# Weight-part buffers 64 bytes longer, and half the software DMA scratch, in a two-layer hybrid trunk

## The chip, the core and the metric

The kernel runs on one core of a Trainium2 chip. Its time is the device time of one launch in microseconds, the median of three runs: 2938.9 us (2937.18 to 2940.47). On the core, TensorE (PE) multiplies matrices, VectorE (DVE) and ScalarE (ACT) work element by element, GpSimd (POOL) and SyncE (SP) here issue transfers. SBUF is the working memory of 128 partitions, and an address below is a byte offset within a partition. PSUM is the memory that TensorE writes.

## The reference

Each of two layers takes x of 256 tokens by 2048 features, all in float32, and computes

```
h  = rms_norm(x);  [c_q | c_kv,k_pe | u | gates] = h @ W_in
a  = latent attention(c_q, c_kv, k_pe), 16 heads, block-causal, then @ w_o
s  = GLU(gelu(diagonal state-space scan of u))         # S5, 64 groups x 64 states
m  = sigmoid(g_a) * a + sigmoid(g_b) * s
x  = x + rms_norm(m @ W_out)
x  = x + rms_norm((silu(h2 @ W_gate) * (h2 @ W_up)) @ W_down),  h2 = rms_norm(x)
```

The hidden width of the last line is 5632. All weights of a layer are read once.

## The kernel before, in words

All products with weights keep the activations stationary (128 features by 128 tokens are loaded into the array as `lhsT`) and stream the weights (`rhs`, 128 rows by 512 columns). float32 accuracy is had from three products of a type called float32r: each operand is split into a high and a low part, and the result is high·high + high·low + low·high. `gemm` (from line 413 of the kernel before) issues these three for every 128 features and each of the two blocks of 128 tokens; lines 444, 445 and 446 are the three matmuls, with the moving operands `hi`, `lo`, `hi`. Before each matmul stands its weight load (row PEld in the trace).

The weights come through class `Weights`. A tile is 128 partitions by 1024 float32 (two slices of 512 columns): SP fetches it into `raw` (4 buffers), ACT rounds it into `hi` (6 buffers, line 187), DVE subtracts to get `lo` (5 buffers; every DVE instruction shows the counting wrapper's line 151). All three sorts are taken from one pool, `wp`, buffer after buffer, each 4096 bytes long. One weight tile serves twelve matmuls: two slices, two token blocks, three products.

The stationary operands are `H` (the normalized features, then the attention's output; products u, ckv, cq, gates, w_o, FFN gate and up), `uz` (state-space branch; GLU), `mT` (merged branches; W_out) and `aT` (FFN hidden; W_down). Each holds the high and the low half, in blocks of 128 columns, 512 bytes. In the attention's projections the roles are turned for q and k: the weight parts are stationary and the latents `cqT` and `ckvT` are streamed, 256 columns at a time (lines 1306 to 1308 and 1333 to 1335); for v (lines 1351 to 1353) the weight parts are streamed again, 256 columns.

The order of the instructions is written out by the program itself: `Background` sets pieces of the state-space scan and of the transposes between the matmuls, by counts of steps and by an account of DVE's time. No address goes into it. Buffers are laid out pool after pool: the scratch of the software DMAs (those that POOL issues) from address 0, then the small constants, `cp`, `wp`, `hp` (`H`), `xp`, `vp`, and the pools of the stage.

Of the kernel before, what the change touches and what calls it, by code (L numbers as in the profile page):

```python
# [42 lines left out]
NXO, NB5 = 2, 2  # L43
NEG = float(np.finfo(np.float32).min)
# [29 lines left out]
class Background:  # L74
    """Work set between the matrix products: pieces due some steps later, and generators, which go on
    as long as the vector engine's work so far would be done LEAD ns after the tensor engine's."""
# [31 lines left out]
    def spread(self, g):  # L108
        """one piece of g at each step"""
        for _ in g:  # L110
            yield from self.wait(1)
# [28 lines left out]
class Counted:  # L140
    """an engine whose instructions' times are added up in the background's clock"""
# [14 lines left out]
class Weights:  # L156
    """Weights in the order in which they are used: fetched ahead, split ahead into two float32r parts."""
# [21 lines left out]
    def high_to(self, i):  # L179
        self.fetch_to(self.ns + self.nraw - 1)  # L180
        while self.nh <= min(i, self.ns + self.nraw - 1, self.pos + self.nhigh - 1, len(self.plan) - 1):
            n = self.nh
            _, _, a, b, parts = self.plan[n]
            h = self.pool.tile([128, 1024], F32R, tag="hi", name=f"hi{n}", bufs=self.nhigh)
            hv = h[:, 0:a * b].rearrange("p (a b) -> p a b", a=a)
            for src, dst in parts or self.whole:
                self.nc.scalar.activation(out=dst(hv), in_=src(self.raw[n]), func=AF.Copy)  # L187
            self.high[n] = hv
            self.nh += 1

    def split_to(self, i):
        while self.ns <= min(i, self.pos + self.nlow - 1, len(self.plan) - 1):
            n = self.ns
            self.high_to(n)
            _, _, a, b, parts = self.plan[n]
            raw, hv = self.raw.pop(n), self.high.pop(n)
            l = self.pool.tile([128, 1024], F32R, tag="lo", name=f"lo{n}", bufs=self.nlow)
            lv = l[:, 0:a * b].rearrange("p (a b) -> p a b", a=a)
            for src, dst in parts or self.whole:
                self.vector.tensor_tensor(  # L200
                    out=dst(lv), in0=src(raw), in1=dst(hv).bitcast(F32), op=ALU.subtract
                )
            self.done[n] = (hv, lv)
            self.ns += 1
        self.fetch_to(self.ns + self.nraw - 1)

    def get(self, n, key, ahead):
        """weights n now, the parts of those up to 'ahead' begun"""
        assert self.plan[n][0] == key, (self.plan[n][0], key)
        begun = self.nh - 1  # L210
        self.high_to(max(n, ahead))
        self.split_to(max(n, min(begun, ahead)))
        return self.done[n]
# [7 lines left out]
def trunk_kernel(ctx: ExitStack, tc: tile.TileContext, a: dict, out: bass.AP, cst: bass.AP,  # L221
# [19 lines left out]
    def T(pool, shape, tag, dt=F32, **kw):  # L241
        cnt[0] += 1
        return pool.tile(list(shape), dt, tag=tag, name=f"{tag}_{cnt[0]}", **kw)

# [41 lines left out]
    def rms_part(o, ss, width):  # L286
        """o = what the sums of squares in the columns of ss, but for the last, and eps have in the argument of rms"""
        n = ss.shape[1]
        V.tensor_reduce(out=o, in_=ss[:, 0:n - 1], axis=AX.X, op=ADD)
        tsc(o, o, 0.5 * RMS_GAIN / width, MUL, 0.5 * RMS_GAIN * EPS, ADD)  # L290

    def rms(o, part, last, width, between=()):
        """o = 1 / sqrt(mean + eps) for one block of tokens: a first guess by its bits (negative, of 3.375 times the
        result), one step of third order and one of second; 'between' fills the vector engine's waits"""
        h, z = T(vp, [128, 1], "rms_h", bufs=2), T(vp, [128, 1], "rms_z", bufs=2)
        between = list(between)
        for f in (
            lambda: stt(h, last, 0.5 * RMS_GAIN / width, part, MUL, ADD),
            lambda: tsc(o.bitcast(I32), h.bitcast(I32), -0.5, MUL, RMS_GUESS, ADD),
            lambda: stt(z, o, o, h, MUL, MUL),  # L300
            lambda: stt(z, z, -5.0 / 3.0, z, ADD, MUL),
            lambda: stt(o, z, 1.25, o, ADD, MUL),
            lambda: stt(z, o, o, h, MUL, MUL),
            lambda: stt(o, z, -2.0 / 3.0, o, ADD, MUL),
        ):
            f()
            if between:
                between.pop(0)()

    def rms_steps(o, ss, width):  # L310
        """the same for both blocks of tokens, as separate pieces"""
# [101 lines left out]
    def gemm(key, nk, lhs, n, done, before=None, after=None, first=4):  # L413
        """out[token block] = lhs.T @ weights; 'before' opens on one token block and then the other, 'after' closes so"""
# [46 lines left out]
    ACT.dma_start(out=cs, in_=cst)  # L461
    ident, rperm = cs[:, 0:128], cs[:, 128:256]
# [6 lines left out]
    def put_blocks(d, srcs, evac):  # L469
        """four transposes into one bank, some steps from now, and then the pieces that take them from there"""  # L470

        def first():
            ps = aux()
            for i, x in enumerate(srcs()):
                transpose(ps[:, 128 * i:128 * i + 128], x)
            bg.chain(1, evac(ps))

        bg.later(d, first)

    def put_pairs(d, dst, f0, src):  # L480
        """two column blocks of src [tokens, tb, n], transposed and split into dst"""
# [73 lines left out]
    def warm(f):  # L555
        """the table of an activation function, loaded before it is needed"""
        act(junk()[:, 0:1], zero, f)
# [4 lines left out]
    zero = T(vp, [128, 1], "zero")  # L562
    V.memset(ap=zero, constant=0.0)
# [8 lines left out]
    class Features:  # L572
        """x [128 tokens, tb, D], times the gain of each feature, as [128 features, hi/lo, k, tokens]"""
# [10 lines left out]
        def ev_high(self, tb, q):  # L584
            """the high parts; returned are the low ones, still to do"""
# [12 lines left out]
        def pair(self, k):  # L598
            """features k and k + 1 of both token blocks: the transposes, and what takes them from there"""
# [8 lines left out]
    def opening(f, stats, tail=None):  # L608
        """what the first product with these features has before its steps"""
# [53 lines left out]
    def boundary(pool, xsrc, xdst, gsrc, key, nk, lhs, gains):  # L663
        """x + norm(lhs @ w) * gain, chunk after chunk; with gains, the new x goes on to the next product"""
# [34 lines left out]
        def tail(what, q=None):  # L699
            """the last steps of token block 'what', or the second one's scale, the first one's features among it"""  # L700
# [62 lines left out]
    def s5_seeds(l, q, tab, par, ldt, smi, ang, tmp):  # L763
        """decay, cos and sin of theta 2^(k-1), and the zero-order hold's factors, by channel"""
# [26 lines left out]
        # zero-order hold: f = (abar - 1) / a  # L791
# [23 lines left out]
    def s5_base(tab, c1, eb, room):  # L815
        """exp(i theta (t + 1/2)), t < 32, for the channel tiles from c1 on"""
# [24 lines left out]
    def s5_ahead(l, scr):  # L841
        """the next layer's tables, by way of DRAM"""
# [12 lines left out]
    for l in range(depth):  # L855
# [4 lines left out]
        # ------------------------------------------------------------ u  # L860
# [13 lines left out]
        # ------------------------------------------------------------ S5  # L874
        def s5(l=l, gains=gains):
# [45 lines left out]
            # the frame's phase is exp(i theta (t - 127.5)): the second half by doubling, the first its mirror image  # L921
# [34 lines left out]
            def prep(ft, craw):  # L956
                """block-diagonal lhsT of this feature tile: B as [(c g p), (g n)], C as [(g n), (c g p)]"""
# [46 lines left out]
            def gelu(ft, g):  # L1004
                """tanh-form gelu of y + D u, split into uz"""
# [94 lines left out]
        def begin(prev=prev, l=l):  # L1100
            """room for this layer, once the last product before it has let go"""
# [16 lines left out]
        # ------------------------------------------------------------ u  # L1118
# [12 lines left out]
        # ------------------------------------------------------------ c_kv | k_pe  # L1131
# [14 lines left out]
        def put_norm(d, v, n):  # L1146
            """v [128 tokens, tb, n] scaled to unit mean square, from step d on"""
# [43 lines left out]
        # ------------------------------------------------------------ gates  # L1191
# [26 lines left out]
        # ------------------------------------------------------------ latent attention, two heads at a time  # L1218
# [139 lines left out]
        # ------------------------------------------------------------ w_o, gated  # L1358
# [22 lines left out]
        # ------------------------------------------------------------ GLU of the S5 branch, merge  # L1381
# [3 lines left out]
        def begin_glu():  # L1385
            """the S5 branch done to its end, and its room taken over"""
            nonlocal gp, mT, sub
            bg.finish()
            sub.close()
            sub = ExitStack()  # L1390
            gp = sub.enter_context(tc.tile_pool(name=f"glu{l}", bufs=1))
            mT = T(gp, [128, 2, KD, S], "mT", F32R)
            warm(AF.Sigmoid)
# [35 lines left out]
        # ------------------------------------------------------------ w_out, residual  # L1429
# [4 lines left out]
        # ------------------------------------------------------------ SwiGLU  # L1434
# [68 lines left out]
```

## Time and profile before

| what | value |
|---|---|
| median of three runs | 2938.9 us |
| span of the profiled execution | 2934.7 us |
| median less that span | 4.2 us |
| TensorE busy (matmuls) | 2902.1 us, 99% of the span |
| VectorE busy | 1902.7 us, 65% |
| ScalarE busy | 1413.1 us, 48% |
| chain that ended last | 96% on TensorE |
| HBM traffic | 188 GB/s over the span |

The span runs from the first to the last instruction of the program; the 4.2 us between it and the median are the launch's edges and the difference between executions, and the page gives no other time of the profiled execution. A matmul's duration in the trace is the time from its start to the modelled end of its last column, and successive matmuls overlap; what a matmul costs in a dense stretch is the distance from its start to the start of the next, called the pitch here. The timeline's first column gives the starts. A window's row gives busy us (and count) of PE, PEld, DVE, ACT and POOL in this order, then the granted clock, the DMA share and GB/s.

### The profile page before, as it was taken

How to read it: one execution, taken by the hardware profiler on the slowest of the kernel's cores; microseconds unless marked ns; L12 is line 12 of the kernel's file. 1: busy time of each engine (PE TensorE's matmuls, PEld its weight loads, DVE VectorE, ACT ScalarE, POOL GpSimd, SP SyncE). 2: the span in 40 equal slices, each digit the busy share in tenths (PEclk: the TensorE clock that was granted, in tenths of full speed). 3: DMA queues.
4: the chain of work that ended last, by engine and by line, in shares of the span. 5: the costliest groups of instructions: out<-in, count | busy, mean ns of one | idle time of the engine just before them, and what ended most of it. 6: DMA issues, size and time to landing. Idle time of an engine off the chain costs nothing.

```text
span 2934.7 us, 37400 instructions
## 1 busy us (share of the span) xinstructions
PE 2902.1 (99%) x13557; PEld 2350.9 (80%) x13557; DVE 1902.7 (65%) x2988; ACT 1413.1 (48%) x2343; POOL 33.1 (1%) x65
## 2 busy tenths in 40 slices
PE   8999999999999999999999999999999999999998
PEld 7777887787788888888877778878878888888887
DVE  7888998765765554544478888986665554454444
ACT  6655665444544444333366556644445444444333
POOL 0000000000000000000000000000000000000000
PEclk9999999999999999999999999999999999999999
DMA  7666335666666666655576663357666566666554
GB/s 220 200 197 185 110 117 180 210 214 202 216 204 202 188 192 193 189 192 192 173 228 195 193 187 112 116 182 240 214 205 206 180 193 195 185 187 229 190 192 142
DMA packets 311222, 553.77 MB, mean 189 GB/s; under 512 B 44353, under 2 KB 57085, under 8 KB 310653
## 3 DMA queue, kind: packets, MB, share of 16 engines
q1 hardware_dynamic: 301708, 528.43, 57.8%
q0 software_dynamic: 4544, 14.42, 1.5%
q10 hardware_dynamic: 4784, 8.53, 0.8%
q8 instruction: 106, 1.74, 0.2%
q14 instruction: 80, 0.65, 0.1%
HBM read 532.74 MB, written 18.56 MB: 188 GB/s over the span
## 4 chain that ended last, share of the span: by engine, by line
PE 96%; DVE 2%; DMA 1%; ACT 0%; issue 0%; SPq 0%; DVEq 0%; ACTq 0%
PE acc L444 28%; PE acc L446 28%; PE acc L445 28%; PE y L1001 2%; PE aux L467 2%; PE bu L991 1%; PE acc L1306 1%; PE acc L1308 1%; PE acc L1307 1%; DVE lo L151 1%; PE bu L992 1%; PE bu L993 1%; PE aux L1286 0%; PE aux L1237 0%; PE aux L1238 0%
## 5 line engine op out<-in xcount | busy, mean ns | idle before, releaser
L151 DVE TENSOR_TENSOR lo<-raw,hi 128x1024 fp32r<-128x1024 f32 (+3 forms) x992 | 1147.8, 1172 | 620.9 <-PE acc L445 413.4
L187 ACT ACTIVATE hi<-raw 128x1024 fp32r<-128x1024 f32 (+3 forms) x992 | 994.1, 1018 | 748.6 <-PE acc L446 573.7
L444 PE MATMUL acc<-hi,H 128*128 128x512 f32 (+1 forms) x2432 | 963.7, 396 | 0.4 <-ACT X L264 0.3
L446 PE MATMUL acc<-hi,H 128*128 128x512 f32 (+1 forms) x2432 | 945.0, 389 | 4.6 <-DVE H L151 4.6
L445 PE MATMUL acc<-lo,H 128*128 128x512 f32 (+1 forms) x2432 | 944.4, 388 | 1.2 <-DVE lo L151 1.2
L444 PEld LDWEIGHTS acc<-hi,H 128*128 128x128 f32 x2432 | 457.2, 188 | 108.2 <-issue 13.2
L446 PEld LDWEIGHTS acc<-hi,H 128*128 128x128 f32 x2432 | 457.0, 188 | 103.5 <-DVE H L151 8.8
L445 PEld LDWEIGHTS acc<-lo,H 128*128 128x128 f32 x2432 | 457.7, 188 | 90.0 <-DVE lo L151 2.6
L444 PE MATMUL acc<-hi,aT 128*128 128x512 f32 x704 | 278.7, 396 | 0.0
L445 PE MATMUL acc<-lo,aT 128*128 128x512 f32 x704 | 278.4, 395 | 0.0
L446 PE MATMUL acc<-hi,aT 128*128 128x512 f32 x704 | 278.4, 395 | 0.0
L446 PEld LDWEIGHTS acc<-hi,aT 128*128 128x128 f32 x704 | 132.3, 188 | 32.0
L444 PEld LDWEIGHTS acc<-hi,aT 128*128 128x128 f32 x704 | 132.4, 188 | 31.8
L445 PEld LDWEIGHTS acc<-lo,aT 128*128 128x128 f32 x704 | 132.4, 188 | 31.8
L444 PE MATMUL acc<-hi,uz 128*128 128x512 f32 x256 | 102.4, 400 | 1.6 <-ACT uz L264 1.6
L444 PE MATMUL acc<-hi,mT 128*128 128x512 f32 x256 | 101.4, 396 | 0.0
L446 PE MATMUL acc<-hi,uz 128*128 128x512 f32 x256 | 101.2, 395 | 0.0
L445 PE MATMUL acc<-lo,uz 128*128 128x512 f32 x256 | 101.2, 395 | 0.0
L446 PE MATMUL acc<-hi,mT 128*128 128x512 f32 x256 | 100.9, 394 | 0.0
L445 PE MATMUL acc<-lo,mT 128*128 128x512 f32 x256 | 100.9, 394 | 0.0
L264 ACT ACTIVATE X<-acc,rstd 128x512 f32<-128x512 f32 (+1 forms) x64 | 41.2, 651 | 121.0 <-PE acc L446 119.4
L264 ACT ACTIVATE aT<-aux 128x512 fp32r<-128x512 f32 x44 | 26.1, 598 | 146.2 <-PE aux L467 146.2
(194 smaller groups left out, 2702.8 us busy)
## 6 DMA issues: line engine op xcount, KB each, us to landing
raw<-in_w_in_dram SPq DMA_DIRECT2D x176, 512.0 KB, 4.3
raw<-in_w_ffn_gate_dram SPq DMA_DIRECT2D x176, 512.0 KB, 4.2
raw<-in_w_ffn_up_dram SPq DMA_DIRECT2D x176, 512.0 KB, 3.8
raw<-in_w_ffn_down_dram SPq DMA_DIRECT2D x176, 512.0 KB, 4.4
raw<-in_w_o_mla_dram SPq DMA_DIRECT2D x64, 512.0 KB, 4.0
raw<-in_w_glu_dram SPq DMA_DIRECT2D x64, 512.0 KB, 4.9
raw<-in_w_out_dram SPq DMA_DIRECT2D x64, 512.0 KB, 4.7
raw<-in_w_uq_dram SPq DMA_DIRECT2D x32, 384.0 KB, 3.6
```

What stands on the lines that cost most here:

```text
L151: return f(**kw)
L187: self.nc.scalar.activation(out=dst(hv), in_=src(self.raw[n]), func=AF.Copy)
L264: ACT.activation(out=o, in_=x, func=f, **kw)
L444: PE.matmul(out=o, lhsT=xh, rhs=h[:, kk], start=(k == 0), stop=False)
L445: PE.matmul(out=o, lhsT=xh, rhs=lo[:, kk], start=False, stop=False)
L446: PE.matmul(out=o, lhsT=xl, rhs=h[:, kk], start=False, stop=(k == nk - 1))
L467: PE.transpose(o, x, ident[0:rows, 0:rows])
L991: PE.matmul(out=o, lhsT=bd[r, 0, i], rhs=uh, start=True, stop=False)
L992: PE.matmul(out=o, lhsT=bd[r, 1, i], rhs=uh, start=False, stop=False)
L993: PE.matmul(out=o, lhsT=bd[r, 0, i], rhs=ul, start=False, stop=True)
L1001: PE.matmul(out=yo, lhsT=cm[:, i, c].rearrange("p g q -> p (g q)"), rhs=xx[:, i], start=(i == 0), stop=(i == 1))
L1306: PE.matmul(out=o, lhsT=hi, rhs=cqT[:, 0, k], start=(k == 0), stop=False)
```

## The change

The `hi` and `lo` buffers become 4160 bytes long in place of 4096, of which the last 64 are unused. Three unused pieces (352 bytes ahead of `wp`, 320 ahead of `H`, 480 in `vp`) move what follows them, and the scratch of the software DMAs shrinks from 16384 to 8192 bytes, which makes room. Comment strings were replaced by blank lines, so that line numbers stay within a few of the old ones.

```diff
+SHIFT = 16
...
-            h = self.pool.tile([128, 1024], F32R, tag="hi", name=f"hi{n}", bufs=self.nhigh)
+            h = self.pool.tile([128, 1024 + SHIFT], F32R, tag="hi", name=f"hi{n}", bufs=self.nhigh)
             hv = h[:, 0:a * b].rearrange("p (a b) -> p a b", a=a)
...
-            l = self.pool.tile([128, 1024], F32R, tag="lo", name=f"lo{n}", bufs=self.nlow)
+            l = self.pool.tile([128, 1024 + SHIFT], F32R, tag="lo", name=f"lo{n}", bufs=self.nlow)
...
+    def spare(pool, n):
+
+        T(pool, [128, n // 4], "spare")
...
     ACT.dma_start(out=cs, in_=cst)
+    spare(cp, 352)
+    spare(hp, 320)
...
     zero = T(vp, [128, 1], "zero")
+    spare(vp, 480)
...
-    nc = _bacc.Bacc("TRN2", target_bir_lowering=False, num_devices=1)
+    nc = _bacc.Bacc("TRN2", target_bir_lowering=False, num_devices=1, dynamic_dma_scratch_size=8192)
```

No instruction is added, removed or moved: on every engine the list of instructions and of the semaphores that they wait for is the same as before, but for line numbers and tile numbers. What differs is where buffers lie. Start addresses modulo 512 bytes:

| buffers | before | after |
|---|---|---|
| `raw`, 4 | all 160 | all 0 |
| `hi`, 6 | all 160 | 0, 64, 128, 192, 256, 320 |
| `lo`, 5 | all 160 | 384, 448, 0, 64, 128 |
| `H` | 160 | 0 |
| `uz`, `mT`, `aT` | 224 | 32 |
| `cqT`, `ckvT`, layer 0 | 0 | 320 |
| `cqT`, `ckvT`, layer 1 | 352 | 160 |

The second slice of 512 columns of a weight tile lies 2048 bytes on, and a block of 128 stationary columns 512 bytes on, so that both keep the residue of their buffer.

## Rows read from the trace of the kernel before

**Rows 1.** The page: span, TensorE's busy time, granted clock by slice

```profile
span 2934.7 us, 37400 instructions
PE 2902.1 (99%) x13557; PEld 2350.9 (80%) x13557; DVE 1902.7 (65%) x2988; ACT 1413.1 (48%) x2343; POOL 33.1 (1%) x65
...
PEclk9999999999999999999999999999999999999999
```

**Rows 2.** Waits of TensorE, longest first: total us, times, longest

```profile
PE aux L467 <- DVE X L151: 6.8, 6, 1.7
```

**Rows 3.** Groups by line and form: count, busy us, mean ns, idle before

```profile
L445 PE MATMUL acc<-lo,H 128*128 128x512 f32 x2368 | 924.6, 390 | 1.2 <-DVE lo L151 1.2
...
L445 PE MATMUL acc<-lo,aT 128*128 128x512 f32 x704 | 278.4, 395 | 0.0
...
L445 PE MATMUL acc<-lo,uz 128*128 128x512 f32 x256 | 101.2, 395 | 0.0
...
L445 PE MATMUL acc<-lo,mT 128*128 128x512 f32 x256 | 100.9, 394 | 0.0
```

**Rows 4.** Timeline, TensorE: first and last matmul of two unbroken stretches

```profile
1003.37 0.48 PE L444 MATMUL acc<-hi,H 128*128 128x512 f32 x1
...
1045.42 0.39 PE L446 MATMUL acc<-hi,H 128*128 128x512 f32 x1
...
2679.05 0.48 PE L444 MATMUL acc<-hi,aT 128*128 128x512 f32 x1
...
2925.30 0.40 PE L446 MATMUL acc<-hi,aT 128*128 128x512 f32 x1
```

**Rows 5.** Timeline, just after an interruption: second matmul, next weight load, twelfth matmul

```profile
138.56 0.40 PE L445 MATMUL acc<-lo,H 128*128 128x512 f32 x1
138.57 0.19 PEld L446 LDWEIGHTS acc<-hi,H 128*128 128x128 f32 x1
...
140.89 0.39 PE L446 MATMUL acc<-hi,H 128*128 128x512 f32 x1
```

**Rows 6.** Timeline, TensorE: second and last matmul of five unbroken stretches

```profile
65.87 0.31 PE L445 MATMUL acc<-lo,H 128*128 128x320 f32 x1
...
76.14 0.31 PE L446 MATMUL acc<-hi,H 128*128 128x320 f32 x1
...
403.74 0.28 PE L1307 MATMUL acc<-cqT,lo 128*128 128x256 f32 x1
...
406.37 0.28 PE L1308 MATMUL acc<-cqT,hi 128*128 128x256 f32 x1
...
409.12 0.28 PE L1352 MATMUL acc<-lo,ckvT 128*128 128x256 f32 x1
...
410.30 0.28 PE L1353 MATMUL acc<-hi,ckvT 128*128 128x256 f32 x1
...
1797.16 0.28 PE L1307 MATMUL acc<-cqT,lo 128*128 128x256 f32 x1
...
1799.75 0.28 PE L1308 MATMUL acc<-cqT,hi 128*128 128x256 f32 x1
...
1842.23 0.28 PE L1307 MATMUL acc<-cqT,lo 128*128 128x256 f32 x1
...
1844.74 0.28 PE L1308 MATMUL acc<-cqT,hi 128*128 128x256 f32 x1
```

**Rows 7.** VectorE: one group in layer 0, in layer 1; busiest window

```profile
L151 DVE TENSOR_TENSOR P<-E,Z 128x512 f32<-128x512 f32 x64 | 42.6, 708 | 0.0
...
L151 DVE TENSOR_TENSOR P<-E,Z 128x512 f32<-128x512 f32 x64 | 42.5, 707 | 0.0
...
1760.00:1900.00 140.00, 139.60 (x931) 121.45 (x930) 128.82 (x301) 93.60 (x278) 0.00 (x0) 1.00 0.36 111
```

**Rows 8.** POOL's timeline at a layer's middle; the chain there

```profile
727.32 0.55 POOL L684 DMA_DIRECT2D xo<-in_x_dram  x1 [4.79 <-DVE X L151]
...
727.32 5.78 DMA xo<-in_x_dram
```

## The prediction, made before the changed kernel was run

> **What bounds the kernel now.** I read the page first. [...] The waits of TensorE come next: the longest group in all is 6.8 us in six waits [rows 2]. So nothing feeds TensorE too late, and the time is the sum of its pitches, the distances from one matmul's start to the next. Only what alters a pitch can move the end by more than a few microseconds.
>
> The change alters no instruction, so the question is whether a pitch depends on an address. The grouped rows say that it does. The same matmul, 512 columns of `lo` against 128 by 128 stationary, lasts 390 ns where the stationary tile is `H` and 395, 395 and 394 ns where it is `aT`, `uz` and `mT` [rows 3]. In starts: 186 matmuls on `H` take (1045.42 - 1003.37) / 185 = 227.3 ns each, 1056 on `aT` take (2925.30 - 2679.05) / 1055 = 233.4 ns [rows 4]. The three slower tiles have nothing in common but their residue: they start at 224 modulo 512, `H` at 160, and the streamed weights always at 160.
>
> What runs beside a matmul is the weight load of the next one; it begins 0.01 us after the matmul [rows 5]. Both read SBUF. I therefore take as the variable the offset: start of the block being loaded less start of the operand being streamed, modulo 512. It is 0 for `H` and 64 for the other three.
>
> [...]
> [...]
> [...]
> [...]
>
> [...]
>
> **The change part by part.**
>
> *The stationary and streamed starts.* After the change the offset differs from buffer to buffer. For `H` it is 0, 448, 384, 320, 256 or 192 beside a `hi` (two of three matmuls) and 128, 64, 0, 448 or 384 beside a `lo`. So 0 comes in 1/9 + 1/15 = 18% of matmuls and 64 in 7%. For `aT`, `uz` and `mT` it is 32, 480, 416, 352, 288, 224 and 160, 96, 32, 480, 416: never 64. Of most of these offsets no row shows the cost. [...]
>
> `H` has 3 x 2368 = 7104 matmuls of 512 columns, the other three 3 x (704 + 256 + 256) = 3648 [rows 3].
> - `H`: (225.3 - 227.3) x 7104 = -14.2 us. Bounds: -6.6 ns and +6.1 ns each, -47 and +43 us.
> - `aT`, `uz`, `mT`: (225.3 - 233.4) x 3648 = -29.5 us. Bounds: -12.7 ns each, -46 us, and 0.
> - Attention's 960 matmuls of 256 columns: layer 0 from about 12.5 to 12, layer 1 from about 9.3 to 12, 480 each: +1.1 us. Bounds: -3 and +9 us.
>
> Sum: -43 us. From the span 2934.7 that gives 2891.7, and with the 4.2 us between span and median, 2896. With all lower bounds 2843, with all upper ones 2991.
>
> *The split on ACT and DVE.* They read `raw` and write `hi` and `lo` at new residues. A DVE product of 512 elements has 708 ns in layer 0 and 707 in layer 1 [rows 7], where its operands lie 352 apart modulo 512; I take 0. They are hidden behind the matmuls anyhow, but not with much to spare in attention: there DVE is busy 128.8 of 140 us [rows 7]. A TensorE faster by 2% would need the same DVE work in 137 us, which still fits. If it didn't, what is late next is `lo`, and the gain of those two windows, some 5 us, is lost.
>
> *The halved scratch.* POOL issues its software DMAs in 0.55 us each; the reload of `xo` at the middle of a layer takes 5.78 us and lies on the chain [rows 8]. Three of the four boundaries have such reloads. If half the scratch made one of them wait a second landing at each boundary, it would be 3 x 5.8 = 17 us more; at best it is nothing. The issues there are 2.7 to 6 us apart but for four at the start, so I take 0 and keep the 17 us in the range.
>
> [...]
>
> **The rivals.**
>
> *The stream never settles (slower).* After each interruption the pitch isn't at once that of rows 4: in the eleven matmuls after the first of a new stretch it is (140.89 - 138.56) / 10 = 233.0 ns [rows 5], at the same offset 0, and 227.3 is what long stretches come down to. So the excess depends on a phase too, which the equal offsets of all buffers let settle. With the change the offset jumps between `hi` and `lo` at every matmul and with every new weight tile, each twelve matmuls. If the phase never settles, `H` goes to 233.0: +5.7 x 7104 = +40 us, the others gain 0.4 x 3648 = 1.5 us; 2938.9 + 39 = 2978. It decides as soon as the mean pitch of all 10752 matmuls is above (7104 x 227.3 + 3648 x 233.4) / 10752 = 229.4 ns. For it: the unsettled rows. [...]
>
> [...]
>
> *The offset is not the cause.* The difference of rows 4 belongs to the tiles in some other way (their place in SBUF, their writers), or gains and losses cancel: 2933 to 2945. [...]
>
> **How the numbers follow.** Less than 0.2%, 6 us, can't be told from no change. Forecast (gain of 20 to 70 us, 2870 to 2920): 0.50. Full alignment, or near it: 0.16. No change: 0.10. Unsettled, wholly or in part, with or without a wait for scratch: 0.24. So faster 0.66, same 0.10, slower 0.24. The time is that of the forecast, 2896, with 2870 to 2920 as its own range. The range for 8 in 10 goes down to 2850, short of the full-alignment end, and up to 2962, half-way into the unsettled case.
>
> **What would show it.** In the trace after: the pitch of long stretches on `aT` well under 233.4, near 225, and differing from weight tile to weight tile in a pattern with the periods 6 and 5 of the buffers; `H` near 225 and not above 227; the attention about as before; instruction counts, DVE and ACT means unchanged; waits for `xo` of the old length. Wrong, if `aT` keeps its 233, if `H` shows 230 or more in the stretches that now have 227.3, or if the gain in pitch is there and comes back as waits of TensorE for `lo`.

## The result: 24 us slower, all of it in the pitch on H

| | before | after |
|---|---|---|
| median of four runs | 2938.9 us (2937.2 to 2940.5) | 2962.7 us (2961.6 to 2964.6) |
| span of the profiled execution | 2934.7 us | 2959.9 us |
| TensorE busy (matmuls) | 2902.1 us | 2928.5 us |

The ratio after to before is 1.0087, with a 95% interval of 1.0075 to 1.0099. The forecast was 2896 us, a gain of 43 us; the time came out 24 us slower and 0.65 us above the upper end of the range.

The page of the changed kernel first. Its lines are span, busy time of each engine with the number of instructions, and TensorE's granted clock by slice; they answer to [rows 1].

```profile
span 2959.9 us, 37400 instructions
PE 2928.5 (99%) x13557; PEld 2353.7 (80%) x13557; DVE 1902.8 (64%) x2988; ACT 1413.8 (48%) x2343; POOL 33.1 (1%) x65
...
PEclk9999999999999999999999999999999999999999
```

The counts are the same, and DVE and ACT are busy for as long as before. Only TensorE's busy time grew, by 26.4 us. The clock has a 9 (90% or more) in every slice as before, but a window of this trace shows what the slices hide (rows of TensorE alone: its busy us and count, granted clock, DMA share, GB/s):

```profile
735.00:739.00 4.00, 1.91 (x9) 1.00 0.68 250
739.60:743.10 3.50, 3.38 (x11) 0.51 0.95 339
```

From 739.6 to 743.1 us the granted clock was 0.51; ahead of it, from 735 to 739 us, TensorE was busy for 1.9 of 4 us. The trace of before has no such stretch between its first 15 us and its last matmul. Six matmuls on `H` took 1.2 us more there than the same six before, which is no effect of the addresses.

The waits of TensorE (total us, times, longest) show that nothing came late in exchange; the second line is the one of [rows 2], now 5.4 us:

```profile
PE aux L474 <- DMA nat<-in_pre_mix_norm_dram: 5.9, 1, 5.9
PE aux L474 <- DVE X L152: 5.4, 5, 1.9
PE acc L451 <- DVE H L152: 5.2, 4, 2.1
```

So the time is in the matmuls themselves. The groups by line and form (count, busy us, mean ns), which answer to [rows 3]:

```profile
L450 PE MATMUL acc<-lo,H 128*128 128x512 f32 x2368 | 932.0, 394 | 1.2 <-DVE lo L152 1.2
...
L450 PE MATMUL acc<-lo,aT 128*128 128x512 f32 x704 | 278.3, 395 | 0.0
...
L450 PE MATMUL acc<-lo,uz 128*128 128x512 f32 x256 | 101.2, 395 | 0.0
L450 PE MATMUL acc<-lo,mT 128*128 128x512 f32 x256 | 101.2, 395 | 0.0
```

The slow tiles stayed at 395 ns; the fast one, `H`, went from 390 to 394. The starts say the same, over the two stretches of [rows 4], again 186 and 1056 matmuls:

```profile
1011.45 0.48 PE L449 MATMUL acc<-hi,H 128*128 128x512 f32 x1
...
1054.29 0.39 PE L451 MATMUL acc<-hi,H 128*128 128x512 f32 x1
...
2704.66 0.48 PE L449 MATMUL acc<-hi,aT 128*128 128x512 f32 x1
...
2950.48 0.39 PE L451 MATMUL acc<-hi,aT 128*128 128x512 f32 x1
```

On `H` it is (1054.29 - 1011.45) / 185 = 231.6 ns, 227.3 before; on `aT` (2950.48 - 2704.66) / 1055 = 233.0, 233.4 before. Summed over the trace, start to next start, all pitches together grew by 25.0 us, and the span by 25.1. The 7104 matmuls on `H` grew by 27.9 us, 1.2 of them by the clock (mean 233.1 to 237.0 ns with the interruptions, 227.7 to 231.4 where the pitch is under 300); `aT`, `uz` and `mT` gave back 1.7 us together, the transposes 1.1 us, and the attention's 960 products took 0.4 us more.

Sorted by offset, the changed kernel shows something that the prediction had not reckoned with. On `H` the mean pitch is 231.3 ns at offset 0, 230.8 at 64, 231.7 at 128, 232.1 at 192, 230.7 at 256, 231.6 at 320, 231.8 at 384 and 231.3 at 448. A matmul's own offset hardly tells there: the 1227 matmuls (those with a pitch under 300 ns) at offset 0, the only offset of `H` before, cost 231.3 ns and not 227.7.

The terms costed at nothing stayed at nothing. The subtraction that makes a whole `lo` tile lasts 1222 ns before and after, the product of [rows 7] 709 in both layers together, and POOL issues the reload of `xo` in 0.55 us as in [rows 8]:

```profile
L152 DVE TENSOR_TENSOR lo<-raw,hi 128x1024 fp32r<-128x1024 f32 x912 | 1103.7, 1222 | 632.5 <-PE acc L450 427.7 <-ACT hi L188 140.7 <-issue 57.8
L152 DVE TENSOR_TENSOR P<-E,Z 128x512 f32<-128x512 f32 x128 | 85.2, 709 | 0.0
...
730.37 0.55 POOL L692 DMA_DIRECT2D xo<-in_x_dram  x1 [4.77 <-DVE X L152]
```

### The profile page after: what moved, and what is told of

The parts are those of the page before. It is cut to its first block, busy times and chain, and to the rows that moved or that the text cites. A ratio compares the mean times of both kernels' runs of the same rounds, so it can differ in the third digit from the quotient of the medians.

```text
span 2959.9 us, 37400 instructions
## 1 busy us (share of the span) xinstructions
PE 2928.5 (99%) x13557; PEld 2353.7 (80%) x13557; DVE 1902.8 (64%) x2988; ACT 1413.8 (48%) x2343; POOL 33.1 (1%) x65
## 4 chain that ended last, share of the span: by engine, by line
PE 96%; DVE 2%; DMA 1%; ACT 1%; SPq 0%; issue 0%; DVEq 0%; ACTq 0%
PE acc L449 28%; PE acc L451 28%; PE acc L450 28%; PE y L1009 2%; PE aux L474 2%; PE bu L999 1%; PE acc L1314 1%; PE acc L1315 1%; PE acc L1316 1%; DVE lo L152 1%; DMA xo<-x 1%; PE bu L1000 1%; PE bu L1001 1%; PE aux L1294 0%; PE aux L1245 0%; PE aux L1246 0%
```

## The experiments

Diffs are against the changed kernel, except for the first. Only the ninth alters instructions, and the seventh gives `lo` a sixth buffer; in all others nothing but addresses differs. "Settled" means the mean pitch from the thirteenth matmul of a stretch on, over all stretches of 40 or more matmuls on that tile. It is a little below the mean of a whole stretch, whose first pitch is 314 to 335 ns in most.

**Is it the scratch?** The kernel before, with half the software DMA scratch and nothing else.

```diff
-    nc = _bacc.Bacc("TRN2", target_bir_lowering=False, num_devices=1)
+    nc = _bacc.Bacc("TRN2", target_bir_lowering=False, num_devices=1, dynamic_dma_scratch_size=8192)
```

> The kernel before with nothing changed but the software DMA scratch, 8192 bytes in place of 16384: every buffer moves down by 8192, a multiple of 512, so all residues modulo 512 stay. If the 24 us of the change come from the residues of the streamed operands (settling: a stretch reaches its low pitch only when all streamed operands have one residue), this is 2939 +/- 3 us, with 227.3 ns on H. If they come from POOL's transfers waiting for scratch, it is 2950 to 2963 us.

Measured: 2937.6 us, ratio to before 1.000 (0.999 to 1.0009). `H` settles at 226.7 ns here as before. The scratch has no part in it.

**All starts equal.** Buffers of the old length, every weight part, `H`, `uz`, `mT` and `aT` at residue 0.

```diff
-SHIFT = 16
+SHIFT = 0
...
-    spare(hp, 320)
...
+            if (480, 480)[l]:
+                spare(mp, (480, 480)[l])
             uz = T(mp, [128, 2, 8, S], "uz", F32R)
...
+            if (480, 480)[l]:
+                spare(fp, (480, 480)[l])
             aT = T(fp, [128, 2, KF, S], "aT", F32R)
```

> The changed kernel with the 64 bytes taken out again: all raw, hi, lo at residue 0, and the stationary tiles H, uz, mT, aT at residue 0 too, so every offset in the products is 0 and every start lies on a multiple of 64. Settling, with the level set by the fixed offset: 227.3 ns on all four tiles; against before that is (227.3 - 233.4) x 3648 = -22 us, 2917 us. If the tile and not the offset made aT slow: H 227.3, aT 233.4, 2939 us. If starts on multiples of 64 are cheaper by themselves: 220 to 223 ns on all, about 2870 us. If the low pitch of H needs starts 32 beyond a multiple of 64: 231 ns on all, 2960 us.

Measured: 2914.3 us, ratio 0.992 (0.9906 to 0.9935). The timeline of TensorE, the same two stretches:

```profile
997.75 0.48 PE L449 MATMUL acc<-hi,H 128*128 128x512 f32 x1
...
1039.80 0.40 PE L451 MATMUL acc<-hi,H 128*128 128x512 f32 x1
...
2661.30 0.48 PE L449 MATMUL acc<-hi,aT 128*128 128x512 f32 x1
...
2900.53 0.39 PE L451 MATMUL acc<-hi,aT 128*128 128x512 f32 x1
```

`H` is back at 42.05 / 185 = 227.3 ns, and `aT` falls to 239.23 / 1055 = 226.8. All four tiles settle at 226.7. So the tile has nothing to do with it, and before and this kernel agree on `H` at different absolute starts (160 and 160, 0 and 0): what counts is the difference of the starts, which the fixed offsets below bear out at 64. Offset 0 keeps 226.7 where the offset stays put.

**Buffers longer by 512 bytes**, so that they are longer and yet keep their residue. Against the changed kernel:

```diff
-SHIFT = 16
+SHIFT = 128
...
-    spare(hp, 320)
```

> The changed kernel with the buffers of the weight parts 512 bytes longer in place of 64: successive buffers are displaced, but all hi and lo keep residue 0, H is at 0, and uz, mT, aT at 32 as in the changed kernel. Settling: H back at 227.3 ns, -26 us against the changed kernel; uz, mT, aT at one fixed offset 32, settled at a level not known, 220 to 233 ns, so 2890 to 2939 us. If any displacement of successive buffers disturbs the stream: H 231 ns, about 2962 us.

Measured: 2939.4 us, ratio 1.0006 (0.9997 to 1.0016). TensorE's timeline:

```profile
1002.69 0.48 PE L449 MATMUL acc<-hi,H 128*128 128x512 f32 x1
...
1044.74 0.40 PE L451 MATMUL acc<-hi,H 128*128 128x512 f32 x1
...
2681.78 0.48 PE L449 MATMUL acc<-hi,aT 128*128 128x512 f32 x1
...
2928.03 0.40 PE L451 MATMUL acc<-hi,aT 128*128 128x512 f32 x1
```

`H` is at 227.3 ns with the longer buffers: the loss hangs on the residues, not on the length. `aT`, here at the constant offset 32, is at 246.25 / 1055 = 233.4, as it was at 64.

**The price of a fixed offset.** All streamed starts at residue 0, and the stationary tiles at one offset each.

```diff
-SHIFT = 16
+SHIFT = 0
...
-    spare(hp, 320)
+    spare(hp, 64)
...
+            if (32, 224)[l]:
+                spare(mp, (32, 224)[l])
...
+            if (64, 64)[l]:
+                spare(gp, (64, 64)[l])
...
+            if (160, 352)[l]:
+                spare(fp, (160, 352)[l])
```

> All hi and lo at residue 0, and the stationary tiles each at another offset: H 64 in both layers; in layer 0 uz 128, mT 192, aT 256; in layer 1 uz 320, mT 384, aT 448. Settling with a level by the fixed offset: H at 233.4 ns like aT before, the other six at levels between 220 and 234 ns that differ from each other, 256 near 227 and 320 lowest, 220. If one residue for all streamed operands is enough, whatever the offset: all at 227.3 ns. If the tile made the difference: H 227.3 and the other three 233.4 ns in both layers.

Measured: 2962.1 us in a single run. The timeline shows `H` at offset 64, then `aT` of layer 0 at 256, `uz` of layer 1 at 320, and `aT` of layer 1 at 448 (186, 1050, 114 and 1056 matmuls):

```profile
1016.51 0.48 PE L449 MATMUL acc<-hi,H 128*128 128x512 f32 x1
...
1059.76 0.40 PE L451 MATMUL acc<-hi,H 128*128 128x512 f32 x1
...
1240.62 0.50 PE L449 MATMUL acc<-hi,aT 128*128 128x512 f32 x1
...
1478.55 0.39 PE L451 MATMUL acc<-hi,aT 128*128 128x512 f32 x1
...
2015.31 0.40 PE L449 MATMUL acc<-hi,uz 128*128 128x512 f32 x1
...
2041.68 0.40 PE L451 MATMUL acc<-hi,uz 128*128 128x512 f32 x1
...
2709.27 0.48 PE L449 MATMUL acc<-hi,aT 128*128 128x512 f32 x1
...
2950.85 0.40 PE L451 MATMUL acc<-hi,aT 128*128 128x512 f32 x1
```

That is 233.8, 226.8, 233.4 and 229.0 ns. `H`, the fast tile of before, is now as slow as `aT` was then, and `aT` is fast at 256. Settled, the offsets give (0 is from the second experiment):

| offset | 0 | 64 | 128 | 192 | 256 | 320 | 384 | 448 |
|---|---|---|---|---|---|---|---|---|
| ns | 226.7 | 233.3 | 232.4 | 228.9 | 226.7 | 233.4 | 232.4 | 228.9 |

The second half repeats the first: the price goes by the offset modulo 256. None of these offsets is cheaper than 0. At 64 `H` has, with starts 64 and 0, the price that `aT` had before with 224 and 160. `raw`, `hi` and `lo` lie at residue 0 here as in the second experiment, so what ACT, DVE and the DMAs write there isn't what makes the pitches differ.

The trace of this run also shows, at one place, `H` at offset 64 while a clock of 0.53 was granted (first the window's row, then the first and the last of seven matmuls in succession):

```profile
749.70:753.00 3.30, 3.30 (x10) 0.53 0.47 185
...
749.63 0.63 PE L449 MATMUL acc<-hi,H 128*128 128x512 f32 x1
...
752.19 0.63 PE L449 MATMUL acc<-hi,H 128*128 128x512 f32 x1
```

That is (752.19 - 749.63) / 6 = 426.7 ns; over this run as a whole, at a mean clock of 0.998, `H` settles at 233.3. The changed kernel has 427 ns too in its stretch at 0.51: four pitches in succession there (741.05 to 742.76 us) are 426 to 427 ns each, though the offset changes between `hi` and `lo`. No row here shows offset 0 at the lower clock.

**Buffers longer by 256 bytes**, the stationary tiles at 0 or 256, to test that period with starts that do change from buffer to buffer.

```diff
-SHIFT = 16
+SHIFT = 64
...
-    spare(hp, 320)
...
+            if (480, 480)[l]:
+                spare(mp, (480, 480)[l])
...
+            if (480, 480)[l]:
+                spare(fp, (480, 480)[l])
```

> Buffers of the weight parts 256 bytes longer in place of 64: hi and lo lie at residues 0 and 256 by turns, all stationary tiles at 256, so the offset jumps between 0 and 256. The run with several fixed offsets had the same settled pitch at 0 and 256, at 64 and 320, at 128 and 384, at 192 and 448. If the pitch knows addresses modulo 256 only, nothing jumps for it: 226.7 ns settled on all four tiles and 2914 us, as with all at residue 0. If a jump modulo 512 disturbs the phase: 231 ns and 2955 to 2963 us.

Measured: 2913.5 us, ratio 0.992 (0.9905 to 0.9935). The stretch on `aT` in layer 1, first and last of 1056 matmuls:

```profile
2661.99 0.48 PE L449 MATMUL acc<-hi,aT 128*128 128x512 f32 x1
...
2901.22 0.39 PE L451 MATMUL acc<-hi,aT 128*128 128x512 f32 x1
```

That is 239.23 / 1055 = 226.8 ns, and all four tiles settle at 226.7. Starts that jump by 256 cost nothing.

**Does the jump itself cost?** All `hi` at residue 0 and all `lo` at 64, so that the offset changes twice in each group of three matmuls, to values whose fixed price is known.

```diff
-SHIFT = 16
+SHIFT = 0
...
+            if n == 0:
+                self.pool.tile([128, 16], F32R, tag="gap", name="gap")
...
-    spare(hp, 320)
+    spare(hp, 448)
...
+            if (416, 416)[l]:
+                spare(mp, (416, 416)[l])
...
+            if (128, 128)[l]:
+                spare(gp, (128, 128)[l])
...
+            if (96, 96)[l]:
+                spare(fp, (96, 96)[l])
```

> All hi at residue 0, all lo at 64; the offset jumps within each group of three matmuls and in the same way in all of them. Offsets beside hi and lo: H 0 and 448, uz 448 and 384, mT 64 and 0, aT 128 and 64. If each matmul has the pitch of its own offset (levels measured with fixed offsets: 0 226.7, 64 233.3, 128 232.4, 192 228.9 ns modulo 256): H (2 x 226.7 + 228.9) / 3 = 227.4, uz 230.1, mT 231.1, aT 232.7 ns, in sum 2938 us. If a jump at each matmul keeps the phase from settling: 231 to 232 ns on all, 2961 us. If a phase is kept and a regular jump settles to a level of its own: four levels between 220 and 234 that these averages don't give.

Measured: 2961.7 us, ratio 1.0082 (1.0067 to 1.0097). On `H` the offset is 0 for two matmuls of three and 448 for one, and the timeline of 186 matmuls on it reads:

```profile
968.20 0.48 PE L451 MATMUL acc<-hi,H 128*128 128x512 f32 x1
...
1011.19 0.39 PE L453 MATMUL acc<-hi,H 128*128 128x512 f32 x1
```

That is 42.99 / 185 = 232.4 ns; `H` settles at 232.0. If fixed prices added up it would be (2 x 226.7 + 228.9) / 3 = 227.4. So a change of offset between matmuls has a price of its own, 4.6 ns for each matmul here. It isn't always a loss: `mT` (0 and 64) settles at 234.5 where the sum gives 231.1, but `aT` (128 and 64) at 231.1 where it gives 232.7.

**One jump for each twelve matmuls.** 64 bytes longer as in the changed kernel, but `lo` with six buffers like `hi`, and both parts of a weight tile at one residue, so that the offset stays for the twelve matmuls of a tile.

```diff
-            l = self.pool.tile([128, 1024 + SHIFT], F32R, tag="lo", name=f"lo{n}", bufs=self.nlow)
+            if n == 0:
+                self.pool.tile([128, 32], F32R, tag="gap", name="gap")
+            l = self.pool.tile([128, 1024 + SHIFT], F32R, tag="lo", name=f"lo{n}", bufs=6)
...
-    spare(hp, 320)
+    spare(hp, 384)
...
+            if (480, 480)[l]:
+                spare(mp, (480, 480)[l])
...
+            if (480, 480)[l]:
+                spare(fp, (480, 480)[l])
```

> The changed kernel with hi and lo of one weight tile at the same residue (six lo buffers in place of five), 64 further with each tile; all stationary tiles at 256. So the offset stays for twelve matmuls and then jumps by 64. If the levels of the fixed offsets are all there is: (2 x 226.7 + 2 x 228.9 + 232.4 + 233.3) / 6 = 229.5 ns, 2944 us. If each jump costs a new settling of about ten matmuls, and twelve are not enough: 231 to 232 ns, 2960 us, and within a tile the later matmuls are nearer to the level of the offset than the earlier ones.

Measured: 2950.0 us, ratio 1.0045 (1.0028 to 1.0062). A stretch of 186 matmuls on `H`, in the timeline:

```profile
1006.91 0.48 PE L451 MATMUL acc<-hi,H 128*128 128x512 f32 x1
...
1049.70 0.40 PE L453 MATMUL acc<-hi,H 128*128 128x512 f32 x1
```

It has 42.79 / 185 = 231.3 ns, and `H` settles at 230.9; the fixed prices of the six offsets (0, 192, 128, 64, 0, 192 modulo 256) average 229.5. What the 1.4 ns are shows in the long stretch on `aT` in layer 1, where nothing interrupts the order of the tiles. They take the buffers from the highest address down, as their pitches tell, so that the offsets follow each other as 0, 192, 0, 64, 128, 192. Two tiles at offset 0, each behind one at 192: the first and the sixth matmul of the one, the first and the eleventh of the other:

```profile
2705.20 0.39 PE L451 MATMUL acc<-hi,aT 128*128 128x512 f32 x1
...
2706.36 0.39 PE L453 MATMUL acc<-hi,aT 128*128 128x512 f32 x1
...
2710.71 0.40 PE L451 MATMUL acc<-hi,aT 128*128 128x512 f32 x1
...
2713.03 0.39 PE L452 MATMUL acc<-lo,aT 128*128 128x512 f32 x1
```

The one has 1.16 / 5 = 232 ns for five matmuls, the other 2.32 / 10 = 232 ns for ten, and after that each is at 227. Averaged over `aT`'s stretches, these two tiles have 228.8 and 230.8 ns in place of 226.7, and the tile at 192 between them has 230.3 in place of 228.9. The other three are at their fixed price from their first matmuls on: 233.3 at 64, 232.5 at 128, 229.3 at 192 behind 128. So not each jump costs something. Those that do make the pitch late in coming down, by up to ten of a tile's twelve matmuls.

**The other offsets**: is any below 226.7? Streamed starts and `H` at 0; `uz`, `mT`, `aT` at 96, 224, 160 in layer 0 and 16, 96, 240 in layer 1.

```diff
-SHIFT = 16
+SHIFT = 0
...
-    spare(hp, 320)
...
+            if (64, 480)[l]:
+                spare(mp, (64, 480)[l])
...
+            if (64, 32)[l]:
+                spare(gp, (64, 32)[l])
...
+            if (128, 192)[l]:
+                spare(fp, (128, 192)[l])
```

For 16 and 240, `uz` and `aT` also lie 16 bytes further inside a tile that is 64 bytes longer.

> All hi and lo at residue 0, fixed offsets not yet seen: in layer 0 uz 96, mT 224, aT 160; in layer 1 uz 16, mT 96, aT 240; H at 0. Modulo 256 the known levels are 0 226.7, 32 and 64 233.3, 128 232.4, 192 228.9 ns. A level that changes smoothly with the offset: 96 233, 160 230.5, 224 228, 240 227, 16 230. If 226.7 ns is not the floor, one of 224 and 240 is lower; if it is, none is. H 226.7 settled, as a control.

Measured: 2930.7 us in a single run. `aT` at 160 (layer 0, 1050 matmuls) and at 240 (layer 1, 1056):

```profile
1219.54 0.49 PE L449 MATMUL acc<-hi,aT 128*128 128x512 f32 x1
...
1464.40 0.39 PE L451 MATMUL acc<-hi,aT 128*128 128x512 f32 x1
...
2678.58 0.48 PE L449 MATMUL acc<-hi,aT 128*128 128x512 f32 x1
...
2919.56 0.39 PE L451 MATMUL acc<-hi,aT 128*128 128x512 f32 x1
```

That is 233.4 and 228.4 ns. Settled: 96 gives 234.3, 160 and 224 give 233.3, 240 gives 228.3. At 16 the longest stretch settles at 226.7, but the mean over all stretches of that tile is 231.2, so that offset has more than one level. None of the offsets measured is below 226.7.

**Is the price the same for fewer columns?** The forecast took over to 512 columns what [rows 6] shows with 256 and 320; there q of layer 1, 256 columns at offset 320, has (1799.75 - 1797.16) / 22 = 117.7 and (1844.74 - 1842.23) / 22 = 114.1 ns, while 512 columns at 320 have 233.4. As in the second experiment, but `aT` at 64 in layer 0 and at 0 in layer 1, and each product of W_down in two halves of 256 columns (the ones that open an accumulation stay whole).

```diff
+                        halves = ((0, 256), (256, 512)) if key == "down" else ((0, n),)
...
+                        for i, j in halves:
+                            PE.matmul(out=o[:, i:j], lhsT=xh, rhs=lo[:, kk, i:j], start=False, stop=False)
...
+            if (32, 480)[l]:
+                spare(fp, (32, 480)[l])
```

> All starts at residue 0 as in the run with equal zero, but aT of layer 0 at 64, and in W_down each matmul of 512 columns is issued as two of 256, each with its own weight load. [...] If the number of columns decides: about 114 to 118 ns per half in layer 0, 228 to 236 a pair, and 117 to 120 in layer 1 at offset 0. [...] If attention was cheap for another reason, such as which operand is stationary: layer 0 not below 120.

Measured: 2939.0 us in a single run. Each line of the timeline holds two matmuls here; between the first and the last start of each pair of lines lie 512 pitches:

```profile
1218.98 0.40 PE L453 MATMUL acc<-lo,aT 128*128 128x256 f32 x2
...
1279.28 0.40 PE L455 MATMUL acc<-hi,aT 128*128 128x256 f32 x2
...
2675.84 0.40 PE L453 MATMUL acc<-lo,aT 128*128 128x256 f32 x2
...
2737.28 0.41 PE L455 MATMUL acc<-hi,aT 128*128 128x256 f32 x2
```

At offset 64 it is 60.30 / 512 = 117.8 ns, at offset 0 it is 61.44 / 512 = 120.0. With 512 columns it was 233.3 at 64 and 226.7 at 0. The order of the two offsets turns round with the number of columns: two halves take 2.3 ns more than one whole at 64 (235.6 and 233.3), and 13.3 ns more at 0 (240.0 and 226.7).

**The version that beats both.** The second experiment, and in addition the latents of the attention at residue 192, so that its products of 256 columns have offset 64 (q, k) or 192 (v).

```diff
+        spare(ap, (416, 64)[l])
```

> The run with all residues 0, and the latents cqT and ckvT at residue 192 in both layers (they were at 288 and 128), so that q and k have offset 64 modulo 256, where 256 columns had their lowest pitch. q and k: from about 117 and 119 ns to 114 to 116 in both layers, 768 matmuls, -2 to -3 us; v (offset 192) about 117. In sum 2911 to 2914 us. If address residues play no part with 256 columns: the same 117 to 119 ns as there.

Measured: 2911.5 us, ratio 0.9913 (0.9896 to 0.9929). The q products fell from 117.1 and 119.0 ns (layer 0, layer 1) to 115.5 and 115.7, and in the traces the attention's 960 products took 1.4 us less in sum. The 2.8 us between this and the second experiment are less than the intervals can tell apart. What can be told is that the two are 26 and 23 us below before.

## Why the prediction was wrong, point by point

**TensorE bounds, and the time is its sum of pitches: right.** In the result and in each experiment the span follows the pitches, and no wait took their place: TensorE's waits sum to 20 to 24 us in every trace.

**The offset is the variable: right, and now shown.** `aT` goes from 233.4 to 226.8 ns when its offset goes to 0 or 256, and `H` from 227.3 to 233.8 when its offset goes to 64. What reads beside the stream is less certain: that it is the weight load was inferred from the fact that only the difference of the two starts counts, and no run took the load away.

**The pitch of 225.3 ns for all the new offsets: the step that failed.** No row and no run shows this term of the sum, nor the bounds of -6.6, +6.1 and -12.7 ns: they were the author's estimates. They carried the five stretches of [rows 6], four of them with 256 columns, over to 512, as if what a matmul costs beyond its columns hardly depended on their number. The stretches show 146.7 ns with 320 columns (offsets 0 and 256 by turns), and with 256 columns 119.5 ns at offset 160, 118.0 at 352, 117.7 and 114.1 at 320. In the ninth experiment, going from offset 0 to 64 takes a matmul of 256 columns from 120.0 to 117.8 ns; one of 512 goes from 226.7 to 233.3. The 225.3 ns were thus the price of other matmuls. With 512 columns, fixed offsets of 32, 64, 96, 128, 160 and 224 cost 232.4 to 234.3 ns and 192 costs 228.9; offset 0, which `H` had, is the cheapest of those measured, and there was nothing to gain on `H`. The lower bound of the sum fell with it: it puts `H` at 227.3 - 6.6 = 220.7 ns, and no fixed offset was below 226.7. Of the signs that the prediction gave for being wrong, two came: `aT` kept 233.0, and `H` shows 231.6.

**aT, uz, mT, -29.5 us: measured -1.7.** They left offset 64 (233.3 ns) for odd multiples of 32, whose fixed prices are 233.3 (32, 160, 224) and 234.3 (96). Weighted by how often each comes, that makes 233.5; the trace has 232.9. The upper bound given for this term, 0, was the right end.

**H, -14.2 us: measured +27.9.** By the fixed prices of the new offsets `H` would be at 229.9 ns (`hi` 229.5, `lo` 230.7); it settles at 231.4, from 226.7. With these prices in place of 225.3 ns the sum's own term would have been some (229.9 - 226.7) x 7104 = +23 us, as an estimate. So some 3.2 ns of the 4.8 are dearer offsets. The other 1.5 ns, for which the sum had no term at all, are put down to the jumps, whose price the sixth and seventh experiments show. The two parts can't be told apart matmul by matmul: in the changed kernel those at offset 0 pay as much as the rest.

**The rival "The stream never settles": right in place and sign, and in part in its cause.** The loss came on `H`, and the jumps at each matmul and each tile have a price. It took 233.0 ns from the rows just after an interruption, where `H` comes to 231.4; its +40 us on `H` against +27.9 is 12 of the 15 us by which its 2978 was too high. It gave the whole loss to the jumps, though, and by the account above they have about a third of it. "Decides above a mean of 229.4 ns" held. That a phase settles was the author's estimate; the runs show the pitches, and no phase.

**Full alignment (0.16), by which starts on multiples of 64 would be the cheaper ones, and "the offset is not the cause": out.** Starts on multiples of 64 cost 233.3 ns at offset 64, and all starts equal give 226.7 at residue 0 as at 160.

**The attention, +1.1 us: about right.** Its products of 256 columns together took 0.4 us more. That is a sum over 960 matmuls: layer 0 gained a little less than layer 1 lost (q in mean from 119.7 to 117.5 ns, and from 115.1 to 118.5). The 12.5, 9.3 and 12 ns of this term are shown by no run; these pitches stand in their place.

**ACT, DVE and the scratch at nothing: right**, the scratch by its own run.

## What to carry to other kernels

In a dense stream of matmuls, compare starts, not durations, and compare the addresses of what is streamed and what is loaded: here the same starts modulo 256 for all of them took 0.8% off a kernel that kept TensorE busy 99% of its span, and the change, whose starts go on by 64 bytes from buffer to buffer, put 0.9% on it. A price read from one matmul shape is not the price of another, even where it looks like a constant per instruction; if the rows show only another shape, the bound for this one is open on both sides. And before spreading buffers over offsets, ask whether the present offset is the cheapest already and whether the change from one to the next costs something.

## What the runs showed of the hardware that was not expected

- The price of a fixed offset has the period 256 bytes, to within 0.1 ns (0 and 256: 226.7; 64: 233.3 and 320: 233.4; 128 and 384: 232.4; 192 and 448: 228.9).
- It depends on the number of columns, and not in one direction: from offset 0 to 64 it is +6.6 ns with 512 columns (226.7 to 233.3) and -2.2 with 256 (120.0 to 117.8).
- A change of offset can cost beyond the two prices (232.0 where they give 227.4) or save (231.1 where they give 232.7). On its way down to the price of offset 0 the pitch took five matmuls behind one jump and ten behind another.
- At a granted clock of 0.53, 512 columns took 426.7 ns at offset 64, which settles at 233.3 over the whole run (mean clock 0.998); at 0.51 they took 427 at changing offsets, where `H` settles at 231.4 over the whole run (0.999).

Why 256, why the number of columns counts, whether the offset does at the lower clock too, and what it is that settles, no run here shows; that stays open.
